# Encoder layer on one core: operands split in place, weights split later, loads re-placed at two stage borders

## The chip, the core and the metric

The kernel runs on one core of one Trainium2 chip. The metric is the device time of one execution in microseconds (us); lower is better. A core has TensorE (PE, with its weight loads as PEld), VectorE (DVE), ScalarE (ACT), GpSimd (POOL) and SyncE (SP), which here issues nearly all DMAs. Each engine runs its own instructions in the order in which they are written; semaphores make one engine wait for another.

## The reference

One transformer-like encoder layer on 2048 tokens of width 1024. `mlstm_group` is a bidirectional chunkwise mLSTM with 4 heads, `mla_group` a latent attention with 4 heads, and the feed-forward part squares a ReLU.

```python
z = rms_norm(x, g_mix) @ w_in                       # q, k, v, out-gate, gates | latents, rotary key
a = mlstm_group(q, k, v, o, gates, b_gates, g_out)  # sigmoid(o) * normed (forward + backward scan)
b = mla_group(c_q, c_kv, k_pe, cos, sin, ...)       # softmax(q k^T) v over all 2048 tokens
x = x + concat(a, b) @ w_out
x = x + square(relu(rms_norm(x, g_ffn) @ w1)) @ w2  # w1: 1024 x 4096, w2: 4096 x 1024
```

## The kernel before

**Arithmetic.** Every large product is made of three matmuls (`mm3`, lines 63 to 65). An operand is split (`split`, lines 48 and 49): ACT casts it to a rounded high part, DVE or POOL (`eng`) subtracts that from it for a low part. So each new operand tile costs an ACT instruction and a DVE or POOL instruction.

**Stages.** Projections (phase A, its order made by the framework's scheduler) run to about 465 us. From there on each engine's order is as the code is written. The attention loop makes one score product per step `g` and calls `next(work)` once per step, which advances the mLSTM generator (`mlstm_prelude`, `mlstm_steps`) by one `yield`; at its end `drain` (`OutProj.weights`) is advanced instead. Ahead of the loop stand the loads and splits of the first q block and the four k blocks of head 0 (`load_q`, `split_q`, `load_k`, `split_k`, POOL as `eng`). The output projection follows, then the feed-forward part.

**Phase A's last store.** `o` (the out-gate) is stored to `d_sg` from SP (line 454), 16 tiles in all.

**Attention's reciprocals.** `invert` takes the reciprocal of the row sums, writes them to DRAM (`d_rd`, line 1032) and at once loads them back broadcast over the partitions (`rb`, line 1034). SP waits for the store to land ahead of that load.

**Drain** (`weights`, from line 1176). `w_out` comes in 16 raw tiles through 8 stage buffers; ahead of `k == 4` the first two token tiles are loaded (`load_y`, `load_x`), into the ring, which has 8 buffers of one name `r`.

**Feed-forward, first layer** (`layer1`). A two-by-two Strassen scheme with 7 products: tokens come in two halves, `w1` in 16 blocks of 256 columns, so `n` runs from 0 to 31 with 7 products (slots) each; one product is 12 matmuls into a PSUM bank `pu` of 6. For a product, two operands must be there: 7 weight operands per `n` (`w1_split`; four of them combined by POOL from raw blocks, `w1_combine`, line 1358), and 7 token operands per half (`H`), each of four 128x512 pieces, which stay for 16 `n`. In a slot the order of the code is: product, stores, POOL combines of results (line 1452), `evacuate` of the product before it (DVE add, line 1415; ACT relu and square, lines 1418 and 1419), then for the next `n` combines and one split. Seven operands are split before the first product, two before and five behind `open1`.

**Second half of the tokens.** In `n` = 1 to 13 the generator `tokens`, one step per slot, normalises the tokens of the second half (ACT line 1287, POOL 59 and 1288, DVE 1291), transposes them on PE (`dpt`, lines 1300 and 1301), combines them (POOL, 1309) and stores all 7 operands to `d_h`. From `n` = 14 eight pieces are loaded into stage tiles, and in `n` = 15 and 16 `h_pieces` splits piece by piece into the operand tiles, as the first half's last products let go of them: 28 pieces of 128x512, several in one slot.

The second layer (7 products again, accumulated over `f`) is not touched.

## Time and profile before

| | us |
|---|---|
| median of 3 runs | 2686.47 (2686.41 to 2686.77) |
| profiled execution, its own time | 2682.24 |
| its span in the trace | 2680.5 |
| PE busy | 2599.5 (97%) |
| DVE busy | 1571.5 (59%) |
| ACT busy | 1196.0 (45%) |
| POOL busy | 806.6 (30%) |

The profiled execution is read by stretches: a view by windows gives for each the busy time of every engine and the granted TensorE clock. Shares over the whole span say little, since stages differ. The slices of the page in which PE is below nine tenths are four: the first, and those that hold 469 to 536, 1139 to 1206 and 1742 to 1809 us; the borders of the stretches shown further down were put where a stage's first and last instructions lie.

### The profile page before, as it was taken

What the parts mean: (1) busy time and instruction counts of PE and PEld (TensorE: products, weight loads), DVE (VectorE), ACT (ScalarE), POOL (GpSimd) and SP (SyncE); (2) the same over time, 40 slices, a digit from 0 to 9 for tenths busy, and PEclk for the clock granted to TensorE, in tenths of its full rate; (3) what the DMA queues carried; (4) which work ended last, traced back from release to release, by engine and by line L of the source; (5) the groups of instructions that cost most, each with busy time, mean ns of one, the idle gap of its engine ahead of it and who ended that gap; (6) DMA issues with size and microseconds to landing.
All of it is one profiled execution on the core that took longest, in us unless ns stands there. A gap on an engine that the chain in (4) does not pass through costs nothing. (4 is left out here: it accounts for less than half of the span.)

```text
span 2680.5 us, 37472 instructions
## 1 busy us (share of the span) xinstructions
PE 2599.5 (97%) x13227; PEld 2185.9 (82%) x13227; DVE 1571.5 (59%) x2918; ACT 1196.0 (45%) x2469; POOL 806.6 (30%) x738
## 2 busy tenths in 40 slices
PE   8999999899999999989999999989999999999999
PEld 6888887778888888878887777768887888888887
DVE  5585475555666666654366565665554377566443
ACT  6455443445656665652134444555444333322332
POOL 1211210223224232222216655555554023232000
PEclk9999999999999999999999999989999999999999
DMA  4344243255335343245665554654444844444552
GB/s 150 118 132 157 95 135 115 67 133 126 94 92 129 91 111 103 66 132 176 204 221 181 185 169 157 199 170 153 150 152 145 324 142 150 145 142 148 210 173 102
DMA packets 300599, 391.59 MB, mean 146 GB/s; under 512 B 33473, under 2 KB 187388, under 8 KB 300412
## 3 DMA queue, kind: packets, MB, share of 16 engines
q1 hardware_dynamic: 300412, 389.21, 46.3%
q8 instruction: 104, 1.70, 0.3%
q14 instruction: 83, 0.68, 0.1%
HBM read 256.94 MB, written 132.17 MB: 145 GB/s over the span
## 5 line engine op out<-in xcount | busy, mean ns | idle before, releaser
L63 PE MATMUL pd<-w2h,uh 128*128 128x512 f32 x896 | 349.3, 390 | 1.3 <-ACT w2h L48 1.0
L64 PE MATMUL pd<-w2l,uh 128*128 128x512 f32 x896 | 349.3, 390 | 0.9 <-DVE w2l L49 0.9
L65 PE MATMUL pd<-w2h,ul 128*128 128x512 f32 x896 | 349.1, 390 | 0.0
L49 DVE TENSOR_TENSOR ul<-ur,uh 128x1024 fp32r<-128x1024 f32 x110 | 152.7, 1388 | 257.3 <-ACT uh L48 257.3
L49 DVE TENSOR_TENSOR ptl<-ptp,pth 128x512 fp32r<-128x512 f32 x256 | 176.6, 690 | 200.2 <-ACT pth L48 200.1
L48 ACT CAST uh<-ur 128x1024 fp32r<-128x1024 f32 x110 | 115.9, 1054 | 396.0 <-PE pd L64 380.6
L49 DVE TENSOR_TENSOR r<-w1raw,r 128x512 fp32r<-128x512 f32 x160 | 153.5, 975 | 187.2 <-ACT r L48 187.1
L48 ACT CAST pth<-ptp 128x512 fp32r<-128x512 f32 x256 | 149.2, 583 | 254.3 <-PE ptp L1043 254.1
L1418 ACT ACTIVATE e<-e 128x512 f32<-128x512 f32 x128 | 80.9, 632 | 341.7 <-DVE e L1415 341.7
L1452 POOL TENSOR_TENSOR e<-e 128x512 f32<-128x512 f32 x128 | 188.9, 1485 | 126.1 <-ACT e L1419 117.1
L1015 DVE TENSOR_SCALAR_CACHE_REDUCE p<-ps 128x512 f32<-128x512 f32 x256 | 175.2, 684 | 58.9 <-PE ps L1014 57.9
L63 PEld LDWEIGHTS pd<-w2h,uh 128*128 128x128 f32 x896 | 168.3, 188 | 36.9 <-ACT w2h L48 1.4
L64 PEld LDWEIGHTS pd<-w2l,uh 128*128 128x128 f32 x896 | 168.3, 188 | 36.4 <-DVE w2l L49 1.6
L65 PEld LDWEIGHTS pd<-w2h,ul 128*128 128x128 f32 x896 | 168.3, 188 | 34.8
L1415 DVE TENSOR_TENSOR e<-pu,e 128x512 f32<-128x512 f32 x224 | 150.0, 681 | 23.4 <-PE pu L65 21.6
L1043 PE MATMUL ptp<-ident,p 128*128 128x128 f32 x1024 | 154.0, 274 | 0.0
L63 PE MATMUL pz<-wh,hh 128*128 128x512 f32 (+1 forms) x384 | 151.0, 395 | 3.0 <-ACT hh L48 3.0
L64 PE MATMUL pz<-wl,hh 128*128 128x512 f32 (+1 forms) x384 | 151.2, 394 | 0.4 <-DVE wl L52 0.3
L65 PE MATMUL pz<-wh,hl 128*128 128x512 f32 (+1 forms) x384 | 151.4, 394 | 0.0
L63 PE MATMUL pv<-pth,vh 128*128 128x256 f32 x512 | 146.0, 285 | 3.2 <-DVE y L1060 2.0
L1582 POOL TENSOR_TENSOR r<-wr,r 128x512 f32<-128x512 f32 x48 | 79.2, 1650 | 229.6 <-DMA wr<-in_w 149.0
L64 PE MATMUL pv<-ptl,vh 128*128 128x256 f32 x512 | 146.2, 286 | 1.4 <-DVE ptl L49 1.4
(361 smaller groups left out, 6807.2 us busy)
## 6 DMA issues: line engine op xcount, KB each, us to landing
d_u<-e SPq DMA_DIRECT2D x224, 256.0 KB, 2.3
ur<-d_u SPq DMA_DIRECT2D x110, 512.0 KB, 3.6
w1raw<-in_w SPq DMA_DIRECT2D x64, 512.0 KB, 4.7
wr<-in_w SPq DMA_DIRECT2D x96, 256.0 KB, 4.7
raw<-d_h SPq DMA_DIRECT2D x56, 256.0 KB, 4.3
raw<-in_w_in SPq DMA_DIRECT2D x48, 256.0 KB, 2.9
xt<-in_x SPq DMA_DIRECT2D x16, 512.0 KB, 3.6
mb<-d_M SPq DMA_DIRECT2D x32, 256.0 KB, 4.5
```

Of the source, the lines that this page charges most:

```text
L48: nc.scalar.copy(hi, src)
L49: (eng or nc.vector).tensor_tensor(lo, src, hi.bitcast(F32), op=ALU.subtract)
L63: nc.tensor.matmul(out, ah, bh, start=first, stop=False)
L64: nc.tensor.matmul(out, ah, bl, start=False, stop=False)
L65: nc.tensor.matmul(out, al, bh, start=False, stop=last)
L1015: nc.vector.tensor_scalar(probs[b, a][:, j, :], o, SCALE, None, op0=ALU.mult, op1=ALU.max, accum_out=maxes[b, a][:, j:j + 1])
L1043: nc.tensor.transpose(pt[:, k, :], p[:, j, k * P:(k + 1) * P], c.ident)
L1415: nc.vector.tensor_tensor(out, o, t, op=ALU.add)
L1418: nc.scalar.activation(t, t, AF.Relu)
L1452: self.c.nc.gpsimd.tensor_tensor(o, a, b, op=f)
L1582: nc.gpsimd.tensor_tensor(R, wr, R, op=ALU.subtract)
```

## The change

In phase A and the opening of attention: the `d_sg` stores are issued by ACT instead of SP; the first q block and k blocks 0, 1 and 3 are split with DVE instead of POOL; the prelude has two more yields ahead of its transposes, and two yields are taken out elsewhere. In attention, `invert` only stores, and a new `broadcast` loads four steps later. In the drain, `load_y` moves to `k` = 1 and 3, `load_x` to `k` = 6 and 7. The ring has two names, `r0` and `r1`, of 4 buffers each. In `layer1` a weight operand is split three products ahead of its use, ahead of the slot's evacuation; the combines of `w1` and its loads stand in other slots; only one operand instead of five is split behind `open1`; `tokens` has four yields instead of two between normalising and transposing. The second half's operands come by `exchange`: raw data is loaded into the tile of the low part, ACT copies it rounded to the high part, and DVE subtracts in place. Operand 0 uses the 8 stage tiles, operand 1 four ring tiles, and operands 2 to 6 the tiles of the first half's operands 0 to 4, loaded behind product (15, p). It has 4 pieces of 128x512 and 12 of 128x1024, one per slot, from `n` = 14 to 16.

```diff
-            nc.sync.dma_start(c.d_sg[t * P:(t + 1) * P, :], o)
+            nc.scalar.dma_start(c.d_sg[t * P:(t + 1) * P, :], o)
...
         nc.vector.tensor_copy(gs[:, 1:2], cu[:, P - 1:P])
         yield
+        yield
+        yield
...
         def invert(b):
             rd = dens[b]
             nc.vector.reciprocal(rd, rd)
+            nc.sync.dma_start(c.d_rd[b].rearrange("a p -> p a"), rd)
+
+        def broadcast(b):
             dd = c.d_rd[b]
-            nc.sync.dma_start(dd.rearrange("a p -> p a"), rd)
             rb = dens[b] = yp.tile([P, 256], F32, name="rb")
             nc.sync.dma_start(rb, bcast(dd.rearrange("a p -> (a p)"), P))
...
-        split_q(0, 0)
+        split_q(0, 0, nc.vector)
         for j in range(4):
             if j < 3:
                 load_k(0, j + 1)
-            split_k(0, j)
+            split_k(0, j, nc.gpsimd if j == 2 else nc.vector)
...
             if s == 2 and 0 < b <= N:
                 invert(b - 1)
+            if s == 6 and 0 < b <= N:
+                broadcast(b - 1)
...
-            if k == 4:
-                for s in range(2):
-                    self.load_y(s)
-                    self.load_x(s)
-                yield
+            if k in (1, 3):
+                self.load_y(k // 2)
+            elif k > 5:
+                self.load_x(k - 6)
...
     def w1_split(self, n, op):
-        w = self.ring.tile([P, 2, 4, P], F32R, name="r")
+        if (n, op) < (0, 2):
+            w = self.ring.tile([P, 2, 4, P], F32R)
+        else:
+            w = self.ring.pool.tile([P, 2, 4, P], F32R, name="r0")
...
+    def exchange(self):
...
+        def place(hi, lo):
+            nc.scalar.copy(hi, lo.bitcast(F32))
+            nc.vector.tensor_tensor(lo, lo.bitcast(F32), hi.bitcast(F32), op=ALU.subtract)
+
+        def load(hi, lo, src):
+            nc.sync.dma_start(lo.bitcast(F32), src)
+            todo.append((hi, lo))
+
+        first = [[self.stage.tile([P, 512], F32R, name="raw") for _ in range(4)] for _ in range(2)]
+        second = [[self.ring.pool.tile([P, 2, 512], F32R, name="r1") for _ in range(2)] for _ in range(2)]
...
+        for p in range(12):
+            if p < 5:
...
+                for k in range(0, 4, 2):
+                    load(hi[:, k:k + 2, :], lo[:, k:k + 2, :], c.d_h[1, p + 2, :, k:k + 2, :])
+            if p < 7:
+                self.H[p] = nxt[p]
+            place(*todo.pop(0))
+            yield
...
                 normalise(c, self.sp, x, x, [junk, junk])
-                yield
-                yield
+                for _ in range(4):
+                    yield
                 transpose_x(c, self.psT, x, x)
...
-                todo = [(op, k) for op in range(7) for k in range(4)]
-                for _ in range(8):
-                    self.h_load(1, *todo.pop(0))
-                extra = self.h_pieces(1, todo)
+                extra = self.exchange()
             for p in range(7):
                 self.product(n, p)
+                m, q = divmod(7 * n + p + 3, 7)
+                if m < N:
+                    self.w1_split(m, q)
                 self.flush()
...
                 prev = n, p, self.ps
-                if n + 1 < N:
-                    if p == 0:
-                        if n + 2 < N:
-                            self.load_w1(n + 2)
-                        self.w1_combine(n + 1, "S1")
-                        self.w1_combine(n + 1, "S2")
-                    elif p == 2:
+                if p == 0:
+                    self.w1_combine(n, "S4")
+                elif p == 1 and n + 1 < N:
+                    self.w1_combine(n + 1, "S1")
+                    self.w1_combine(n + 1, "S2")
+                elif p == 3:
+                    if n + 2 < N:
+                        self.load_w1(n + 2)
+                    if n + 1 < N:
                         self.w1_combine(n + 1, "S3")
-                    elif p == 4:
-                        self.w1_combine(n + 1, "S4")
-                    if p >= 1:
-                        self.w1_split(n + 1, p - 1)
-                    if p == 6:
-                        self.w1_split(n + 1, 6)
-                if n == 0 or (n == self.NU - 1 and p > 0) or n == self.NU:
-                    next(extra, None)
-                    next(extra, None)
-                    if n and p % 2 == 0:
-                        next(extra, None)
-                elif n < self.NU - 2:
+                next(extra, None)
+                if n == 0:
                     next(extra, None)
...
-                for k in range(2, 7):
-                    if k == 3:
-                        ff.w1_combine(0, "S4")
-                    ff.w1_split(0, k)
+                ff.w1_split(0, 2)
```

How the order moves at three places: first POOL at the opening of attention, between its last memset of the prelude (`v_4980`) and the split of v; `ql`, `kl` and `rl` are the low parts of q, k and the rotary part of k.

```order
 L542 MEMSET v_4980 128x4
-L49 TENSOR_TENSOR ql<-raw,qh 128x512
-L996 TENSOR_TENSOR qr<-raw,qr 64x512
-L49 TENSOR_TENSOR kl<-raw,kh 128x512
-L49 TENSOR_TENSOR rl<-raw,rh 128x512
-L49 TENSOR_TENSOR kl<-raw,kh 128x512
-L49 TENSOR_TENSOR rl<-raw,rh 128x512
-L49 TENSOR_TENSOR kl<-raw,kh 128x512
-L49 TENSOR_TENSOR rl<-raw,rh 128x512
 L49 TENSOR_TENSOR kl<-raw,kh 128x512
 L49 TENSOR_TENSOR rl<-raw,rh 128x512
 L49 TENSOR_TENSOR vl<-raw,vh 128x512 x4
```

Eight subtracts leave POOL; the pair that stays is that of k block 2. On DVE they stand among phase A's last instructions.

Second, SP in the drain, before: `raw` are tiles of `w_out`, `d_ya` and `d_yb` the two halves of the projection's input.

```order
L1184 DMA raw<-in_w_out 128x512 x4
L1032 DMA d_rd<-rd_13181 128x2x1
L1034 DMA rb<-d_rd 128x256
L1184 DMA raw<-in_w_out 128x512 x2
L1063 DMA d_yb<-y 128x256
L1184 DMA raw<-in_w_out 128x512 x2
L1222 DMA r<-d_ya 128x512
L1223 DMA r<-d_yb 128x4x128
```

The same place in the changed kernel:

```order
L1198 DMA raw<-in_w_out 128x512 x2
L1235 DMA r_13345<-d_ya 128x512
L1236 DMA r_13345<-d_yb 128x4x128
L1198 DMA raw<-in_w_out 128x512 x2
L1031 DMA d_rd<-rd_13179 128x2x1
L1198 DMA raw<-in_w_out 128x512 x2
L1065 DMA d_yb<-y 128x256
L1235 DMA r_13401<-d_ya 128x512
L1236 DMA r_13401<-d_yb 128x4x128
L1198 DMA raw<-in_w_out 128x512 x2
L1036 DMA rb<-d_rd 128x256
```

The first `d_ya` load now stands ahead of the store of `d_rd`, and the load of `rb` stands six loads and a store behind that store instead of right behind it.

Third, DVE in `layer1` at the first token tile, before: L1291 is the normalising multiply, L1301 the copy of the transposed tile out of PSUM, L49 the low part of a weight operand, and L1415 an evacuation.

```order
L1291 TENSOR_SCALAR raw<-raw,nr 128x512 x2
L1415 TENSOR_TENSOR e<-pu,e 128x512 x2
L49 TENSOR_TENSOR r<-sw,r 128x512
L1415 TENSOR_TENSOR e<-pu,e 128x512
L49 TENSOR_TENSOR r<-w1raw_15056,r 128x512 x2
L1301 TENSOR_TENSOR raw<-dpt,vec 128x512 x2
L1415 TENSOR_TENSOR e<-pu,e 128x512
```

The same place in the changed kernel (L1304 is the multiply, L1470 the evacuation, L1314 the copy):

```order
L1304 TENSOR_SCALAR raw<-raw,nr 128x512 x2
L49 TENSOR_TENSOR r_15311<-sw,r_15311 128x512
L1470 TENSOR_TENSOR e<-pu,e 128x512 x2
L49 TENSOR_TENSOR r_15331<-w1raw_15112,r_15331 128x512
L1470 TENSOR_TENSOR e<-pu,e 128x512
L49 TENSOR_TENSOR r_15351<-w1raw_15110,r_15351 128x512
L1470 TENSOR_TENSOR e<-pu,e 128x512
L49 TENSOR_TENSOR r_15372<-sw,r_15372 128x512
L1314 TENSOR_TENSOR raw<-dpt,vec 128x512 x2
```

Between the multiply and the copy stand four slots' work instead of two; splits and evacuations alternate as they did.

## Rows read from the trace of the kernel before

**Rows 1.** Windows: stretch; its us; PE, PEld, DVE, ACT, POOL busy (instructions); clock; DMA share; GB/s

```profile
465.50:500.70 35.20, 23.02 (x89) 16.25 (x89) 19.04 (x56) 14.91 (x21) 18.23 (x19) 0.81 0.38 102
1169.30:1199.00 29.70, 18.89 (x119) 16.86 (x116) 16.55 (x31) 17.98 (x35) 12.37 (x10) 0.83 0.61 179
1387.00:1711.90 324.90, 305.63 (x1326) 248.07 (x1325) 199.51 (x251) 148.06 (x272) 193.86 (x157) 0.97 0.53 174
1711.90:1731.20 19.30, 19.30 (x86) 15.78 (x85) 12.84 (x14) 9.81 (x18) 10.63 (x7) 1.00 0.51 156
1731.20:1773.30 42.10, 30.69 (x86) 19.45 (x85) 34.00 (x42) 23.34 (x44) 14.57 (x9) 0.76 0.60 192
1773.30:2063.30 290.00, 290.00 (x1261) 236.84 (x1259) 158.82 (x208) 137.64 (x241) 159.33 (x116) 1.00 0.44 151
...
1653.85:1673.18 19.33, 19.33 (x85) 15.80 (x85) 11.96 (x16) 9.25 (x16) 11.01 (x8) 1.00 0.46 155
```

**Rows 2.** Waits, 440 to 505 us: who waits for whom, total, times, longest

```profile
PE ps L1011 <- POOL kl L49: 5.2, 2, 4.8
...
PE pm L592 <- DVE gs L587: 4.9, 1, 4.9
...
PE ps L1010 <- DVE p L1015: 1.1, 1, 1.1
```

**Rows 3.** Timeline of SP's queue: start, us, instruction

```profile
445.14 22.96 SPq L454 DMA_DIRECT2D d_sg<-vo  x5
468.20 0.38 SPq L952 DMA_DIRECT2D raw<-d_kn  x1
```

**Rows 4.** Timeline of POOL at the opening of attention

```profile
468.96 1.26 POOL L49 TENSOR_TENSOR kl<-raw,kh 128x512 fp32r<-128x512 f32 x1
...
477.59 1.28 POOL L49 TENSOR_TENSOR rl<-raw,rh 128x512 fp32r<-128x512 f32 x1
```

**Rows 5.** Waits, 1169 to 1200 us

```profile
PE pm L1239 <- DMA r<-d_ya: 6.1, 1, 6.1
```

**Rows 6.** Timeline of SP's queue in the drain

```profile
1177.23 0.43 SPq L1032 DMA_DIRECT2D d_rd<-rd  x1
1185.04 0.33 SPq L1034 DMA_DIRECT2D rb<-d_rd  x1
...
1188.10 0.37 SPq L1222 DMA_DIRECT2D r<-d_ya  x1
```

**Rows 7.** Waits, 1387 to 1711 us

```profile
ACT e L1418 <- DVE e L1415: 157.8, 57, 7.8
DVE r L49 <- ACT r L48: 107.8, 58, 5.0
...
PE dpt L1300 <- DVE raw L1291: 19.3, 11, 5.3
DVE raw L1291 <- POOL nr L59: 17.4, 8, 4.0
...
ACT r L48 <- POOL w1raw L1358: 12.5, 3, 5.6
```

**Rows 8.** Timelines of ACT, then DVE, then POOL, 1656 to 1676 us

```profile
1656.14 0.60 ACT L48 CAST r<-sw 128x512 fp32r<-128x512 f32 x1
...
1674.90 0.60 ACT L48 CAST r<-sw 128x512 fp32r<-128x512 f32 x1
...
1656.77 0.69 DVE L49 TENSOR_TENSOR r<-sw,r 128x512 fp32r<-128x512 f32 x1 [1.27 <-ACT r L48]
...
1669.39 1.74 DVE L49 TENSOR_TENSOR r<-w1raw,r 128x512 fp32r<-128x512 f32 x1 [1.88 <-ACT r L48]
...
1669.29 1.29 POOL L1452 TENSOR_TENSOR e<-e 128x512 f32<-128x512 f32 x1
```

**Rows 9.** Groups of DVE's instructions, 1711 to 1773 us: busy, mean ns, idle before

```profile
L49 DVE TENSOR_TENSOR h0l<-raw,h0h 128x512 fp32r<-128x512 f32 x4 | 5.9, 1506 | 0.0
...
L49 DVE TENSOR_TENSOR h5l<-raw,h5h 128x512 fp32r<-128x512 f32 x4 | 2.6, 680 | 0.0
```

More of the change, by code (lines that the diff above doesn't have):

```diff
@@ L956, in load_k, with split_k @@
             kraw[h, j] = raw, rr
-        def split_k(h, j):
+        def split_k(h, j, eng=nc.gpsimd):
             raw, rr = kraw.pop((h, j))
@@ L961, in split_k @@
             kl = kp.tile([P, 512], F32R, name="kl")
-            split(nc, kh, kl, raw, eng=nc.gpsimd)
+            split(nc, kh, kl, raw, eng=eng)
             rh = kp.tile([P, 512], F32R, name="rh")
             rl = kp.tile([P, 512], F32R, name="rl")
-            split(nc, rh, rl, rr, eng=nc.gpsimd)
+            split(nc, rh, rl, rr, eng=eng)
             K[h, j] = kh, kl, rh, rl
@@ L987, in load_q, with split_q @@
             qraw[h, j] = raw, rr
-        def split_q(h, j):
+        def split_q(h, j, eng=nc.gpsimd):
             raw, rr = qraw.pop((h, j))
@@ L992, in split_q @@
             ql = qp.tile([P, 512], F32R, name="ql")
-            split(nc, qh, ql, raw, eng=nc.gpsimd)
+            split(nc, qh, ql, raw, eng=eng)
             qr = qp.tile([P, 512], F32R, name="qr")
             nc.scalar.copy(qr, rr)
-            nc.gpsimd.tensor_tensor(qr[ROPE:P, :], rr[ROPE:P, :], qr[ROPE:P, :].bitcast(F32),
-                                    op=ALU.subtract)
+            eng.tensor_tensor(qr[ROPE:P, :], rr[ROPE:P, :], qr[ROPE:P, :].bitcast(F32), op=ALU.subtract)
             Q[h, j] = qh, ql, qr
@@ L1160, with __init__, tile @@
 UOP = {p[0]: i for i, p in enumerate(PROD2)}
+class Ring:
+    def __init__(self, pool):
+        self.pool, self.n = pool, 0
+    def tile(self, shape, dtype):
+        self.n += 1
+        return self.pool.tile(shape, dtype, name=f"r{self.n % 2}")
 class OutProj:
@@ L1189, in weights @@
         yield
-        self.yp = self.ent_ring(c.tc.tile_pool(name="ring", bufs=8, side="right", reuse_waits="tile"))
+        self.yp = Ring(self.ent_ring(c.tc.tile_pool(name="ring", bufs=4, side="right", reuse_waits="tile")))
         self.wp = self.ent_w(c.tc.tile_pool(name="o_w", bufs=1, side="right", reuse_waits="tile"))
@@ L1219, in load_y @@
         tok = slice(t * P, (t + 1) * P)
-        y = self.yp.tile([P, 2, 512], F32, name="r")
+        y = self.yp.tile([P, 2, 512], F32)
         ya, yb = y[:, 0, :], y[:, 1, :].rearrange("p (k t) -> p k t", k=NH)
@@ L1228, in load_x @@
         t = self.ORDER[s]
-        xt = self.x[s] = self.yp.tile([P, D], F32, name="r")
+        xt = self.x[s] = self.yp.tile([P, D], F32)
         nc.sync.dma_start(xt, c.x[t * P:(t + 1) * P, :])
@@ L1234, in prep_y @@
         ya, yb = self.y.pop(s)
-        yh = self.yp.tile([P, 8, P], F32R, name="r")
-        yl = self.yp.tile([P, 8, P], F32R, name="r")
+        yh = self.yp.tile([P, 8, P], F32R)
+        yl = self.yp.tile([P, 8, P], F32R)
         pt = bank if bank is not None else self.psY.tile([P, 4, P], F32, name="ypt")
@@ L1375, in h_split @@
             pool = self.hp if op < 3 else self.hp1
-            self.H[op] = (pool.tile([P, 4, 512], F32R, name=f"h{op}h"),
-                          pool.tile([P, 4, 512], F32R, name=f"h{op}l"))
+            t = [pool.tile([P, 4, 512], F32R, name=f"h{op}{part}") for part in "hl"]
+            self.H[op] = [[x[:, i, :] for i in range(4)] for x in t]
         hh, hl = self.H[op]
-        split(self.c.nc, hh[:, k, :], hl[:, k, :], raw)
+        split(self.c.nc, hh[k], hl[k], raw)
+    def exchange(self):
+        c, nc = self.c, self.c.nc
+        todo = []
+        def place(hi, lo):
[6 more added lines that the diff above has]
+        second = [[self.ring.pool.tile([P, 2, 512], F32R, name="r1") for _ in range(2)] for _ in range(2)]
+        for k in range(4):
+            load(first[0][k], first[1][k], c.d_h[1, 0, :, k, :])
+            if k % 2:
+                yield
+        for k in range(2):
+            load(second[0][k], second[1][k], c.d_h[1, 1, :, 2 * k:2 * k + 2, :])
+        yield
+        for _ in range(4):
+            place(*todo.pop(0))
+            yield
+        nxt = [first, [[t[:, k, :] for t in s for k in range(2)] for s in second]]
+        for p in range(12):
+            if p < 5:
+                pool = self.hp if p < 3 else self.hp1
+                hi, lo = (pool.tile([P, 4, 512], F32R, name=f"h{p}{part}") for part in "hl")
+                nxt.append([[t[:, k, :] for k in range(4)] for t in (hi, lo)])
+                for k in range(0, 4, 2):
+                    load(hi[:, k:k + 2, :], lo[:, k:k + 2, :], c.d_h[1, p + 2, :, k:k + 2, :])
+            if p < 7:
+                self.H[p] = nxt[p]
+            place(*todo.pop(0))
+            yield
     def h_pieces(self, g, todo):
@@ L1403, in product @@
         for k in range(4):
-            mm3(self.c.nc, o, wh[:, k, :], wl[:, k, :], hh[:, k, :], hl[:, k, :], k == 0, k == 3)
+            mm3(self.c.nc, o, wh[:, k, :], wl[:, k, :], hh[k], hl[k], k == 0, k == 3)
     def slots(self, n):
@@ L1476, in tokens @@
                 normalise(c, self.sp, x, x, [junk, junk])
-                yield
-                yield
+                for _ in range(4):
+                    yield
                 transpose_x(c, self.psT, x, x)
```

## The prediction

> **What bounds the kernel now.** I read the windows first, because the span's mean hides the weak places: PE is busy 97% of it. The reader is to see three stretches in which PE is not full [rows 1]: the opening of attention (465.5 to 500.7, PE 23.02 of 35.2 us at a clock of 0.81), the drain (1169.3 to 1199.0, PE 18.89 of 29.7 us), and the first 17 of 32 steps `n` of the first feed-forward layer (1387.0 to 1773.3, three rows). A step that nothing disturbs takes 19.33 us with PE busy throughout [rows 1], and the 15 later steps take 290.0 us, just 15 times that. The first 17 should then take 17 x 19.33 = 328.6 us; they take 324.9 + 19.3 + 42.1 = 386.3, 57.7 more. PE also makes 64 transposes for the tokens in them. A matmul of 512 columns takes 19.33 / 84 = 0.23 us here and a transpose has a quarter of the columns, so they are worth between 0.06 and 0.23 us each, 4 to 15 us; I take 6.4, near the lower end (an estimate). About 51 us is then idle or slowed time.
>
> Then the waits, stretch by stretch. In the opening PE waits 5.2 us in two waits for POOL's `kl` and 4.9 for `gs` [rows 2]. POOL starts its first `kl` only at 468.96 and ends its last `rl` at 477.59 + 1.28 = 478.87 [rows 4], while SP stands 22.96 us at five `d_sg` stores and issues the next k load at 468.20 [rows 3]. In the drain PE waits 6.1 us for the first `d_ya` tile [rows 5]; SP issues that load at 1188.10, after standing from the `d_rd` store (1177.23) to the `rb` load behind it (1185.04) [rows 6].
>
> In the feed-forward part PE's named waits are for the normalised token (19.3 us, 11 times), which suggests that the transposes come too early. But the same list has no entry of DVE or ACT waiting for PE: the evacuation, which must wait for PE if PE is the bound, never does. ACT waits for DVE's add 157.8 us, DVE for ACT's cast 107.8 [rows 7]. So I read the two as one chain, handing a tile back and forth (cast, subtract, add, relu and square, next cast). From one `n` to the next, the cast of `sw` comes 1674.90 - 1656.14 = 18.76 us later [rows 8], just under PE's 19.33. Seventeen steps of it are 318.9 us, so 386.3 leaves 67.4 us that tokens, exchange and waits put into it. PE stalls only where the lag of this chain shows.
>
> **The opening.** Removed from POOL: three k pairs and the q pair, 8 subtracts of about 1.26 us [rows 4]; they go to DVE among the last work of phase A, at about 0.69 us each [rows 8], 5.5 us beside a full PE. The `d_sg` stores leave SP, so the k and v loads come before the stage rather than at 468.20 [rows 3]. Added to ACT: 16 issues of about 0.33 us [rows 6], 5 us over the whole of phase A, which ACT hides; behind a store there that waits for DVE stands ACT's own next cast, which the PE would see only through phase A's buffers. The weight split there can delay PE; I put 0 to 2 us on that, inside my bound. What is left in the opening: PE's busy 23.02 us at clock 0.81 is 18.6 at full clock. The two `kl` waits (5.2) go. The `gs` wait (4.9) has two more steps ahead of it; at 18.6 / 12 = 1.55 us of PE work in a step (an estimate: some 12 steps stand ahead of the first product with v) 1.8 remain. The wait for a score bank (1.1) [rows 2] may grow as PE comes to it sooner, and so may those behind it in the prelude; I leave 3.3 us for them together. 18.6 + 1.8 + 3.3 = 23.7, so **11.5 us** gained of 35.2; bounds 8 and 14 (the `gs` wait stays whole and the clock half recovers; or the banks cost nothing).
>
> The Trainium skill, page "DMA: Bandwidth & Descriptors", section "Issuing engines are not separate DMA queues", says that issuing from another engine saves only the sequencer's time of issuing; by it moving `d_sg` would be worth nothing here. The row says otherwise for a queue in which a store waits for its data: SP stood 22.96 us at five of them [rows 3].
>
> **The drain.** SP's 7.8 us between 1177.23 and 1185.04 [rows 6] go, and the `d_ya` load stands ahead of the store. PE's wait of 6.1 us [rows 5] then ends by the data before it. What is late next is ACT: it is busy 17.98 of the 29.7 us [rows 1], with 16 casts of `w_out` and the last softmax casts, and cannot end much before 20 us even if it waits only 2. The stretch would go from 29.7 to 22.7, some 3 us above that floor, since the last transposes still wait for it: **7 us**; bounds 3 (the wait moves to ACT) and 9.7 (the floor). The old cover of `broadcast`: it comes four steps later, and the output that uses `rb` is several steps behind it; in the tail of the drain this is the tightest place, and it is inside the lower bound.
>
> **Layer 1, part by part.** Each slot keeps one cast, one subtract and one evacuation, and the split stands ahead of the evacuation instead of behind it. The ring cast, subtract, add, relu, square, cast is the same, and the third piece of order says so: `L49` and `L1470` alternate. So I leave the chain at 18.76 us a step and count what leaves it.
> - The combines now come three or more products ahead of the split that needs them, not about two; ACT's 12.5 us of waits for a POOL combine [rows 7] should go nearly all: 10 us.
> - Four fewer splits stand ahead of the first steps. A split is a cast of 0.60 and a subtract of 0.69 [rows 8], 1.3 us, 5.2 in all, of which I count 3 as exposed at the stage's border. They are not saved, only made later, where PE has a margin.
> - The chain need not have caught up at `n` = 16. The 15 steps behind have 0.57 us of slack each, 8.6 us; I count 4 (an estimate) of it as newly used.
> - The tokens' two more yields move PE's transposes and change nothing in the chain: DVE's wait of 17.4 us for POOL's `nr` [rows 7] stays, because the multiply stands where it stood. What is late next at PE is then a weight, now only three products ahead: it shows after 3 x 2.76 = 8.3 us of lag instead of about 16.
> - The exchange has the same 14,336 columns per partition to cast and subtract; with 1024 columns in one instruction and one in a slot, fewer collide with POOL: 0 to 8 us. I take 0. Its loads wait on SP for product (15, p); queued behind them there are the stores of results and the next `w1` block, both several products early.
>
> 10 + 3 + 4 = **17 us**. The bounds: the combines' gain can be lost to contention (-5), or the waits that I call symptoms may partly be causes (30).
>
> **The sum.** 11.5 + 7 + 17 = 35.5 us. The profiled execution took 2682.24 us; 2682.2 - 35.5 = 2646.7. The median of the runs, 2686.47, is 4.2 above it, so the forecast is 2651.
>
> **Rivals.** *The waits are the bound.* If the chain's rate is not fixed (DVE's 17.4 us for `nr` and the bursts of splits being causes), moving the transposes and spreading the exchange recover all 51 us: 2686.5 - 11.5 - 7 - 51 = 2617. For it speaks that PE names exactly these instructions [rows 7] and that the exchange stretch alone is 42.1 - 19.3 = 22.8 us long; against it, that no evacuation waits for PE. Chance 0.13.
>
> *Nothing comes back in layer 1.* The three-product lead gives PE's stalls to weights, and the combines' wait turns into another; opening and drain alone give 2686.5 - 18.5 = 2668. The form of it in which the change doesn't do what it says belongs here: k block 2 is still POOL's, and ACT may stand behind a `d_sg` store, so that opening and drain give 0 to 5, and the time is within 0.2% of before. Chance 0.18 together, a third of it for the latter.
>
> *The chain becomes longer than PE's step: slower.* A DVE subtract that meets a POOL instruction takes 1.74 us instead of 0.69 [rows 8], and the pieces of operand 0 took 1506 ns against 680 for operand 5 [rows 9]. The change puts other POOL combines beside other subtracts in all 32 steps. Chain 18.76 against 19.33 leaves 0.57 us; one more collision in each step (1.05 us) makes 19.8, two make 20.9. With 32 steps, the kernel loses more than the 35.5 us gained elsewhere from 19.33 + 35.5/32 = 20.4 us a step, and at 20.9 it loses 50: 2686.5 - 35.5 + 50 = 2701. Chance 0.08. The Trainium skill, page "SBUF: State Buffer", section "SBUF: two separate sides", states that DVE and POOL share a port pair that the first holds for its whole instruction while the other fully blocks. The rows agree: the 1.74 us subtract ended 0.55 us after POOL's instruction [rows 8].
>
> **How the numbers follow.** The forecast holds 0.61, with a range of its own of 2633 (14 + 9.7 + 30 gained) to 2676 (8 + 3 + 0, since not all three fall to their lower bound together). The range for all, 2622 to 2676, reaches half way to the first rival and past the second's 2668; left out are the slower rival, the "does not do it" case and half of the first rival, 0.2 together. A measurement of this kernel can tell about 0.2%, 5.4 us, from no change. Faster by more: 0.61 + 0.13 + 0.12 = 0.86; within: 0.06; slower by more: 0.08.
>
> **What would show each step.** In the changed kernel's trace: no wait of PE for `kl` of POOL and an opening of about 24 us; no wait for `d_ya`, a drain of 22 to 23 us; in layer 1 ACT's waits for POOL's combines gone, PE's waits now for weights, still no evacuation that waits for PE, and the first 17 steps at about 369 us. Were evacuations to wait for PE there, and the 17 steps near 335, the first rival would be right. Steps behind `n` = 17 above 19.33 us would show the last rival, and make the prediction wrong.

## The result and the profile after

The changed kernel took 2667.59 us (median of 4 runs, 2663.33 to 2670.84), the kernel before 2686.62 beside it. The ratio is 0.9928, 95% interval 0.9911 to 0.9945: faster by 19 us, and inside the range of the prediction, but some 17 us short of its centre. The profiled execution took 2668.72 us, 13.5 less than that of before. The kernel before had medians from 2681.8 to 2686.6 in the different batches of runs, so below I compare ratios within a batch, and stretches within a trace.

Windows of the changed kernel, columns as in [rows 1]. The first four rows stand for the opening, the drain, and `n` = 0 to 16 in two parts; then come the 15 later steps, and the 17 steps in one row:

```profile
466.30:490.60 24.30, 18.48 (x84) 14.33 (x85) 18.65 (x54) 13.94 (x19) 8.46 (x11) 0.93 0.35 97
1158.30:1188.80 30.50, 19.50 (x123) 17.08 (x121) 17.47 (x32) 18.34 (x39) 12.55 (x10) 0.83 0.71 177
1376.80:1697.60 320.80, 306.57 (x1325) 246.41 (x1324) 205.41 (x245) 147.02 (x271) 199.31 (x156) 0.98 0.53 172
1697.60:1759.00 61.40, 47.69 (x169) 33.67 (x168) 44.79 (x48) 31.46 (x48) 28.23 (x17) 0.92 0.63 205
1759.00:2049.00 290.00, 290.00 (x1261) 236.62 (x1259) 187.07 (x209) 138.16 (x242) 172.16 (x117) 1.00 0.44 144
1376.80:1759.00 382.20, 354.26 (x1493) 280.08 (x1492) 250.20 (x292) 178.48 (x319) 227.55 (x172) 0.97 0.54 177
```

The opening went from 35.2 to 24.3 us, and phase A ends 0.8 later, so 10.1 are won at its end. From the last score product to the first product of the output projection it is 30.5 us, and by the same two marks 30.3 before: nothing. The first 17 steps went from 386.3 to 382.2, 4.1 us. Each other stretch is the same to 1 us, but in the attention loop (from the first product with v to the last score product, 668.0 us before and 667.7 after) that is a loss and a gain in one. PE's idle time ahead of the mLSTM's outer product fell, by rows of before and of after (`issue` is time in which the engine waits for nothing that the profile shows):

```profile
PE pm L691 <- issue: 6.5, 16, 1.2
```

```profile
PE pm L693 <- issue: 1.4, 5, 0.3
```

And just behind the opening's window PE waits for `y`, which waits for `rb`, now loaded later; before, no such wait stands in the loop:

```profile
DVE y L1062 <- DMA rb<-d_rd: 6.4, 1, 6.4
...
PE pv L63 <- DVE y L1062: 5.6, 1, 5.6
```

In the eleven later traces with the changed attention (all below but e4) PE's wait for `y` there is 0.7 to 2.3 us, and the loop takes 661 to 663. So the profiled execution seems to show some 5 us less than the change wins as a rule, which is about what lies between its 13.5 us and the 19 of the medians; a second trace of the changed kernel itself would have to show it. Where the prediction had 11.5, 7 and 17, the trace has 10.1, 0 and 4.

One row tells more than these. In the 15 later steps PE is full in both kernels, but DVE is busy 187.07 us, against 158.82 before [rows 1], for the same instructions. The waits of 1376 to 1678 us (who waits for whom: total, times, longest), 14 steps, which answer to the 15 of [rows 7]:

```profile
ACT e L1473 <- DVE e L1470: 155.2, 53, 9.1
DVE r L49 <- ACT r L48: 81.8, 49, 2.1
...
DVE raw L1304 <- POOL nr L59: 25.2, 8, 4.2
...
PE pu L65 <- DVE r L49: 13.3, 7, 4.0
```

ACT's waits for a combine of POOL are gone, as are PE's for the normalised token. PE now waits for a weight's low part. That is the pattern I expected, yet the time is nearly the same, because the chain itself became slower. ACT's casts of `sw` one step apart (timeline: start, us):

```profile
1851.52 0.62 ACT L48 CAST r<-sw 128x512 fp32r<-128x512 f32 x1
...
1871.03 0.61 ACT L48 CAST r<-sw 128x512 fp32r<-128x512 f32 x1
...
1890.53 0.62 ACT L48 CAST r<-sw 128x512 fp32r<-128x512 f32 x1
```

A step of the chain takes 19.51 us, where [rows 8] had 18.76. That is more than PE's 19.33: from `n` = 17 to 31 the evacuations fall 0.18 us further behind in each step, which the six banks hide until the end. Groups of DVE's subtracts in steps 17 to 30 (busy, mean ns | idle before), before and then after:

```profile
L49 DVE TENSOR_TENSOR r<-w1raw,r 128x512 fp32r<-128x512 f32 x70 | 67.5, 979 | 85.4 <-ACT r L48 85.4
L49 DVE TENSOR_TENSOR r<-sw,r 128x512 fp32r<-128x512 f32 x29 | 25.9, 895 | 19.1 <-ACT r L48 19.1
```

```profile
L49 DVE TENSOR_TENSOR r<-w1raw,r 128x512 fp32r<-128x512 f32 x70 | 85.2, 1217 | 70.3 <-ACT r L48 70.3
L49 DVE TENSOR_TENSOR r<-sw,r 128x512 fp32r<-128x512 f32 x27 | 34.6, 1283 | 26.2 <-ACT r L48 26.2
```

A subtract alone takes 0.69 us [rows 8]. Where it meets POOL it looks like this in the changed kernel (timelines of DVE, then POOL):

```profile
1865.20 1.78 DVE L49 TENSOR_TENSOR r<-w1raw,r 128x512 fp32r<-128x512 f32 x1
...
1863.43 3.00 POOL L1507 TENSOR_TENSOR e<-e 128x512 f32<-128x512 f32 x2 [3.74 <-ACT e L1474]
```

It ends 0.55 us behind POOL's second instruction, as in [rows 8]. So the theory with which I went into the experiments: one chain of DVE and ACT bounds the first half of layer 1 in both kernels, and POOL's combines, which the change moved, lengthen it. Its rivals: the place of the split in the slot lengthens it; or PE's stalls have other causes (tokens, exchange) and the chain is a symptom.

### The profile page after: what moved, and what is told of

It reads as the page before. It is cut to its first block, busy times and chain, and to the rows that moved or that the text cites. A ratio compares the mean times of both kernels' runs of the same rounds, so it can differ in the third digit from the quotient of the medians.

```text
span 2666.9 us, 37134 instructions
## 1 busy us (share of the span) xinstructions
PE 2594.1 (97%) x13227; PEld 2180.9 (82%) x13227; DVE 1615.9 (61%) x2914; ACT 1193.9 (45%) x2457; POOL 826.3 (31%) x730
## 5 line engine op out<-in xcount | busy, mean ns | idle before, releaser
L49 DVE TENSOR_TENSOR ul<-ur,uh 128x1024 fp32r<-128x1024 f32 x110 | 146.9, 1336 | 253.7 <-ACT uh L48 253.5
L49 DVE TENSOR_TENSOR ptl<-ptp,pth 128x512 fp32r<-128x512 f32 x256 | 176.7, 690 | 193.8 <-ACT pth L48 193.7
L49 DVE TENSOR_TENSOR r<-w1raw,r 128x512 fp32r<-128x512 f32 x160 | 187.6, 1173 | 140.8 <-ACT r L48 140.8
L1473 ACT ACTIVATE e<-e 128x512 f32<-128x512 f32 x128 | 80.9, 632 | 346.8 <-DVE e L1470 346.8
L1507 POOL TENSOR_TENSOR e<-e 128x512 f32<-128x512 f32 x128 | 183.4, 1443 | 120.8 <-ACT e L1474 118.2
L1629 POOL TENSOR_TENSOR r<-wr,r 128x512 f32<-128x512 f32 x48 | 87.0, 1813 | 223.3 <-DMA wr<-in_w 141.0
L1470 DVE TENSOR_TENSOR e<-pu,e 128x512 f32<-128x512 f32 x224 | 149.6, 680 | 1.4 <-POOL e L1507 1.2
```

The costliest lines, as they stand in the source:

```text
L49: (eng or nc.vector).tensor_tensor(lo, src, hi.bitcast(F32), op=ALU.subtract)
L1470: nc.vector.tensor_tensor(out, o, t, op=ALU.add)
L1473: nc.scalar.activation(t, t, AF.Relu)
L1507: self.c.nc.gpsimd.tensor_tensor(o, a, b, op=f)
L1629: nc.gpsimd.tensor_tensor(R, wr, R, op=ALU.subtract)
```

## The experiments

**The chain's length.** First the split behind the evacuation again:

```diff
-                if m < N:
-                    self.w1_split(m, q)
...
                 if prev:
                     self.evacuate(*prev)
...
+                if m < N:
+                    self.w1_split(m, q)
```

> The changed kernel with one thing put back: in each slot the weight split stands behind the evacuation again. In the changed kernel the lag of the evacuations behind PE grows by 0.18 us per n from n = 17 to 31, so the chain of DVE and ACT takes 19.33 + 0.18 = 19.51 us per n there; it took 18.76 before. Theory (DVE's subtracts meet POOL's combines more often: 1217 ns instead of 979 for the subtract of a raw weight): the place of the split in the slot changes little, the mean stays above 1100 ns, the lag does not shrink by more than 0.3 us per n, and the time is within 8 us of the changed kernel's 2667.6. Rival (the split ahead of the evacuation makes the hand-off longer): back to 18.76 us per n, the lag shrinks by 0.57 us per n, and the first 17 steps take some 13 us less than 382.2, so about 2655.

2672.17 us, ratio 0.9961 (0.9947 to 0.9976). The subtracts took 1279 and 1253 ns in steps 17 to 30, and the 17 steps 384.0 us. Steps 17 to 31 took 294.6, 4.5 more than in the changed kernel. The rival fell: the order inside the slot did not lengthen the chain, putting it back costs a little. Then the changed kernel without the combines of `w1` from `n` = 2 on, which leaves that part of the computation out:

```diff
     def w1_combine(self, n, name):
...
-        self.c.nc.gpsimd.tensor_tensor(...)
+        if n < 2:
+            self.c.nc.gpsimd.tensor_tensor(...)
```

> The changed kernel without POOL's combines of w1 from n = 2 on (that part of the computation is left out; the splits work on the raw blocks as they are). Theory (contention of DVE's subtracts with POOL sets the chain): the mean subtract falls below 950 ns, the chain to 18.5 us per n or less, the evacuations catch up with PE before n = 31, the first 17 steps take 360 to 372 us instead of 382.2, and the time is 2645 to 2658. Rival (the chain is longer for its order): subtracts and the growth of the lag by 0.18 us per n stay, and the time is within 5 us of 2667.6.

2640.48 us, ratio 0.9843 (0.9829 to 0.9858), 17 steps in 360.3 us, and from `n` = 19 on the lag (from the end of a product to its evacuation) constant, 1.3 to 2.8 us by the slot. So four POOL instructions in a step, for which no cast or subtract of the changed kernel is seen to wait long, cost 22 us of the first 17 steps. Three numbers missed: the subtracts still took 1091 and 1033 ns, not under 950, with the four combines of results still there; the evacuations didn't catch up with PE; and the time lies 4.5 us under the range. Does the place of the combines matter? First those of `w1` moved back:

```diff
-                if p == 0:
+                if p == 0 and n == 0:
                     self.w1_combine(n, "S4")
-                elif p == 1 and n + 1 < N:
-                    self.w1_combine(n + 1, "S1")
-                    self.w1_combine(n + 1, "S2")
-                elif p == 3:
+                if p == 3:
...
                     if n + 1 < N:
-                        self.w1_combine(n + 1, "S3")
+                        self.w1_combine(n + 1, "S1")
+                        self.w1_combine(n + 1, "S2")
+                elif p == 5 and n + 1 < N:
                     self.w1_combine(n + 1, "S3")
+                elif p == 6 and n + 1 < N:
+                    self.w1_combine(n + 1, "S4")
```

> The changed kernel with the combines of w1 in other slots (S1 and S2 in slot 3, S3 in slot 5, S4 in slot 6, so that POOL no longer does six of its eight combines in slots 0 to 2); the hand-off is coupled as in the changed kernel. Theory (where the combines stand decides how many subtracts meet them): the mean subtract falls from 1144 and 1230 ns to 1050 or less, the lag no longer grows behind n = 17, and the first 17 steps take 365 to 376 us, time 2650 to 2662. Rival (only how much POOL does counts, not where): mean above 1100 ns, time within 6 us of 2667.6. Against the theory: the split of S2 now stands two slots behind its combine, and ACT may wait for POOL there.

2677.22 us, ratio 0.9979 (0.9969 to 0.9988), slower than the changed kernel by 0.5%. The mean subtract fell from 1144 and 1230 ns (in the first 17 steps and in the later ones) to 1076 and 1079, not to 1050 as the theory asked; behind `n` = 17 the lag grew by 0.38 us a step, where the theory had it stand still; and a new wait took more than the shorter subtracts gave:

```profile
ACT r L48 <- POOL sw L1371: 23.6, 8, 7.0
```

The 17 steps took 393.6 us: two slots between combine and cast are too few when POOL is behind. So I moved the other four, which nothing waits for soon:

```diff
-                    if p == 1:
+                    if p == 3:
                         self.u_combine(n - 1, "S1")
                         self.u_combine(n - 1, "S2")
-                    elif p == 2:
+                    elif p == 4:
                         self.u_combine(n - 1, "S3")
-                    elif p == 3:
+                    elif p == 5:
                         self.u_combine(n - 1, "S4")
```

> The changed kernel with POOL's combines of results moved from slots 1, 1, 2, 3 to slots 3, 3, 4, 5, so that POOL's eight combines of a step are no longer nearly all in slots 0 to 3; no split waits for these. Theory (where the combines stand decides how many subtracts meet them): mean subtract 1080 ns or less (1144 and 1230 in the changed kernel), the lag no longer grows behind n = 17, the first 17 steps 366 to 377 us instead of 382.3, time 2650 to 2663. Rival (only how much POOL does counts): mean above 1100 ns, the lag grows as before, time within 5 us of 2667.6.

2661.18 us, ratio 0.9922 (0.9908 to 0.9937), which by ratio is the changed kernel again. The subtracts of steps 17 to 30, and DVE's waits in the first 14 steps:

```profile
L49 DVE TENSOR_TENSOR r<-w1raw,r 128x512 fp32r<-128x512 f32 x71 | 63.8, 898 | 80.6 <-ACT r L48 80.4
L49 DVE TENSOR_TENSOR r<-sw,r 128x512 fp32r<-128x512 f32 x28 | 27.7, 988 | 40.0 <-ACT r L48 40.0
```

```profile
DVE r L49 <- ACT r L48: 85.8, 59, 3.0
...
DVE raw L1304 <- POOL nr L59: 26.2, 8, 4.0
...
DVE e L1470 <- POOL e L1507: 8.4, 5, 2.4
```

The subtracts are as short as before the change (984 and 936 ns over all of them in the two parts), and the lag behind `n` = 17 no longer grows (2.4 to 2.9 us): where POOL's work stands does decide how long the chain is there. But the first 17 steps took 380.8 us, not 366 to 377. DVE's wait for `nr` there is what it was (25.2 us after the change); new are some 8 us of waits for POOL's combines of results. What else the shorter subtracts went into stays open. So the collisions explain the later steps; in the first 17 they are not shown to cost much. The time by trace is 7.7 us below that of the changed kernel, but 5.7 of that stand ahead of layer 1, where the two kernels are the same.

**The chain itself.** If one serial hand-off is the bound, cutting it must win more than any of this. ACT's cast stays ahead of the evacuation and DVE's subtract goes behind it (`w1_split` with `True` makes the cast and returns the subtract):

```diff
-                if m < N:
-                    self.w1_split(m, q)
+                sub = self.w1_split(m, q, True) if m < N else None
...
                     self.evacuate(*prev)
...
+                if sub:
+                    sub()
```

> The changed kernel with the hand-off cut in layer 1: in each slot ACT's cast of the weight stands ahead of the evacuation, as it does, and DVE's subtract behind it, so that DVE adds while ACT casts, and neither waits for the other twice in a slot. Theory (one serial chain of cast, subtract, add, relu and square bounds layer 1): the first 17 steps fall from 382.2 to 345 to 360 us, the evacuations stay within about 3 us of PE from n = 18 on, and the time is 2630 to 2648. Rival (PE's stalls come from the tokens' waits and the late exchange loads, not from the chain): within 5 us of 2667.6.

2626.88 us (2626.40 to 2628.09), ratio 0.9795 (0.9779 to 0.9812). The 17 steps took 345.9 us, and from `n` = 18 to 30 the evacuations stayed within 0.7 us of PE; the time was 3 us below what the theory gave. Windows of `n` = 0 to 13 and 14 to 16, and waits in the first:

```profile
1370.50:1648.20 277.70, 277.70 (x1242) 227.64 (x1241) 181.31 (x236) 146.02 (x258) 188.46 (x149) 1.00 0.57 187
1648.20:1716.40 68.20, 62.55 (x253) 49.07 (x252) 51.59 (x57) 40.07 (x62) 38.43 (x24) 0.95 0.69 232
```

```profile
ACT r L1380 <- PE pu L65: 82.2, 58, 3.1
...
ACT e L1480 <- DVE e L1477: 37.9, 23, 4.4
DVE e L1477 <- PE pu L65: 34.2, 35, 1.5
```

PE is full for 277.7 us, and DVE's evacuations wait for PE 35 times. No such wait stood in [rows 7] or after the change. 14 steps of 19.33 are 270.6, so the tokens' transposes cost 7.1 us, near the 6.4 estimated. The cut also shortened the subtracts, from a mean of 1142 ns in the first 14 steps to 942; but e11 had 968 there and took 380.8 us for the 17, so it is the hand-off that counts and not the length of the subtracts. The same cut in the kernel before:

> The kernel before with the same cut in layer 1 and nothing else: casts ahead of the evacuation, subtracts behind it. Theory: the chain was the bound there too, so the first 17 steps fall from 386.3 to 350 to 368 us and the time from 2686.5 to 2652 to 2670. Rival (there the transposes that came too early and the crowded exchange were the bound): the 17 steps stay above 380 and the time above 2680.

The edit is that of e3, for the splits of that kernel. 2647.75 us, ratio 0.9871 (0.9857 to 0.9886), 17 steps in 350.7 us instead of 386.3; the time lies under the theory's range by as much as the kernel before ran faster in this batch (2682.19). The transposes and the crowded exchange stood there unchanged, so they were not the bound: one hand-off was worth 35.6 us in the kernel before, and 36.4 in the changed one (382.3 to 345.9). With it cut, `n` = 14 to 16 take 68.2 us with the new exchange and 70.0 with the old; coupled it was 80.9 and 80.7. The same cut in the exchange, where `finish` subtracts the piece before:

```diff
         def place(hi, lo):
+            finish()
             nc.scalar.copy(hi, lo.bitcast(F32))
-            nc.vector.tensor_tensor(lo, lo.bitcast(F32), hi.bitcast(F32), op=ALU.subtract)
+            behind.append((hi, lo))
```

> The kernel e3_cast_ahead with the same cut made in the exchange: a piece's in-place subtract stands one slot behind its ACT copy, so DVE no longer waits for the copy in the slot. Theory (in the exchange too the hand-off adds up: add, relu, square, copy, subtract in a row are longer than a product): n = 14 to 16 take 60 to 65 us instead of 68.2, time 2619 to 2625. Rival (ACT and DVE are simply full there, 2.8 to 2.9 us of work in a slot of 2.76): 67 us or more, time within 2 us of 2626.9.

2621.96 us (2620.03 to 2627.42), ratio 0.9784 (0.9767 to 0.9801); `n` = 14 to 16 in 63.8 us, of which three steps of PE are 58:

```profile
1647.00:1710.80 63.80, 60.55 (x254) 48.02 (x253) 53.26 (x58) 41.33 (x64) 40.25 (x24) 0.97 0.72 252
```

The step is clear in the trace; by the ratios (0.9795 and 0.9784) it is inside the noise. It is the fastest kernel of this study with e12, below.

**The opening**, on e3. The stores of `d_sg` back on SP, splits as changed:

```diff
-            nc.scalar.dma_start(c.d_sg[t * P:(t + 1) * P, :], o)
+            nc.sync.dma_start(c.d_sg[t * P:(t + 1) * P, :], o)
```

> The kernel e3_cast_ahead with the d_sg stores back on SP, the splits still on DVE. Theory (SP standing at those stores was what kept the k loads back): SP stands some 20 us again, PE waits 3 us or more for k, and the first product with v comes 5 to 10 us later than e3's 488.9, so the time is 2632 to 2637. Rival (the place of the splits alone made the gain): within 2 us of e3's 2626.9.

2627.18 us, ratio 0.9785: no difference, the rival was right. SP stands at the stores as before:

```profile
446.01 16.66 SPq L454 DMA_DIRECT2D d_sg<-vo  x4
464.17 0.57 SPq L658 DMA_DIRECT2D v<-d_v  x1
```

But no k load is behind them: the last load of `d_kn` leaves at 417.76 us, ahead of the stores (468.20 in the kernel before). Then the splits back on POOL:

```diff
-        split_q(0, 0, nc.vector)
+        split_q(0, 0)
-            split_k(0, j, nc.gpsimd if j == 2 else nc.vector)
+            split_k(0, j)
```

> The kernel e3_cast_ahead with the splits of the first q and k blocks back on POOL, the d_sg stores still on ACT. Theory (POOL stands at its memset of qz until the last projection, at about 466 us, so its splits start there however early the data came): PE waits 2 us or more for kl, the first product with v comes 3 to 8 us later than e3's 488.9, time 2630 to 2635. Rival (only the late loads mattered): within 2 us of e3's 2626.9.

2632.08 us, ratio 0.9806 (0.9789 to 0.9822). Against e6, in the same batch, it is 4.9 us slower. The first product with v comes at 497.8 instead of 488.9, 1 us later than the theory's range; counted from phase A's last product it is 33.9 us, against 24.3 and 25.2 in e3 and e6. The last k load leaves late again, at 465.65 us, though no `d_sg` store stands ahead of it on SP: SP's queue waits for POOL's `ql`, which lets go of the buffer. And PE's old wait is there:

```profile
SPq L953 <- POOL ql L49: 22.1, 1, 22.1
```

```profile
PE ps L1011 <- POOL kl L49: 5.3, 2, 4.8
```

So the engine of the splits decides when the k loads leave, not the stores. In the kernel before the same `ql` ended at 467.21 us, 1 us ahead of the load [rows 3]; more the stores can't have cost there:

```profile
465.95 1.26 POOL L49 TENSOR_TENSOR ql<-raw,qh 128x512 fp32r<-128x512 f32 x1
```

By the traces of e7 and e3, 8.9 us at the opening have shrunk to 5.3 at the end. Where the rest went isn't shown: the drain is 1.9 us shorter in e7, but the same code takes 29.0 to 30.9 us there in the nine traces that have it.

**The drain.** In the changed kernel PE's wait there, and what ACT waits for:

```profile
PE pv L63 <- ACT pth L48: 7.4, 3, 6.2
...
ACT woh L48 <- DMA raw<-in_w_out: 5.9, 3, 2.7
```

The last softmax cast (`pth`) stands on ACT behind casts of `w_out` whose data is late:

```profile
1177.38 0.62 ACT L48 CAST woh<-raw 128x512 fp32r<-128x512 f32 x1 [2.65 <-DMA raw<-in_w_out]
...
1182.38 1.27 ACT L48 CAST woh<-raw 128x512 fp32r<-128x512 f32 x2 [2.50 <-DMA raw<-in_w_out]
1183.55 0.58 ACT L48 CAST pth<-ptp 128x512 fp32r<-128x512 f32 x1
```

So, on e3:

```diff
             elif k > 5:
+                if k == 6:
+                    yield
+                    yield
                 self.load_x(k - 6)
```

> The kernel e3_cast_ahead with two more yields in the drain ahead of k = 6, so that the last softmax cast stands ahead of the last four casts of w_out on ACT. Theory (in the changed drain the last product with v waits 6.2 us for a cast that is queued on ACT behind casts of w_out, whose data came 2.65 and 2.50 us late): PE's wait for that cast goes below 1 us, the stretch from the last score product to the first output projection falls from 30.9 us to 25 to 28, and the time is 2 to 6 us below e3's 2626.9. Rival (the transfers themselves are the bound, 5.5 MB in 30 us): the wait moves to the output projection's first tiles, and the time stays within 1.5 us of e3's.

The wait went, and PE waited for `y` instead:

```profile
PE ypt L1255 <- DVE y L1062: 6.0, 1, 6.0
```

27.9 us instead of 30.9 (29.0 to 30.9 in the traces of the unchanged drain), but 2626.94 us, ratio 0.9786, no gain. I took the late broadcast of the last reciprocals for the cause, and replaced its store and load by a matmul of ones with a diagonal, on top of e9 and the two yields:

```diff
...
+            if b == NH * NB - 1:
+                o = psM.tile([P, 512], F32, name="pm")[:, 0:256]
+                nc.tensor.matmul(o, t[:, 0, 0:P], t[:, 1, 0:256], start=True, stop=True)
+                nc.vector.tensor_copy(rb, o)
+                return
```

> The kernel e9_place_behind with the two yields of e5 in the drain, and the last block's reciprocals broadcast by a matmul of ones with a diagonal tile instead of by a store to d_rd and a load. Theory (in e5 PE's wait for the last cast had gone, and in its place PE waited 6.0 us for y, since the store of d_rd took 9.8 us to land among the drain's loads and rb came only after it): that wait goes, the stretch from the last score product to the first output projection falls to 21 to 25 us from e5's 27.9, and the time is 3 to 6 us below e9's. Rival (the transfers are the bound): the output projection's first products wait for w_out or for d_ya instead, and the time is within 1.5 us of e9's.

That reading was wrong. 2623.64 us, ratio 0.9780, a stretch of 28.7 us, and PE still waits for `y`. DVE's timeline of e5 had shown why:

```profile
1178.14 0.69 DVE L49 TENSOR_TENSOR wol<-raw,woh 128x512 fp32r<-128x512 f32 x1 [3.45 <-ACT woh L48]
1179.35 1.34 DVE L49 TENSOR_TENSOR r<-r,r 128x512 fp32r<-128x512 f32 x1 [0.52 <-ACT r L48]
1180.61 0.68 DVE L49 TENSOR_TENSOR r<-pm,r 128x512 fp32r<-128x512 f32 x1
1181.21 0.41 DVE L1062 TENSOR_TENSOR y<-pv,rb 128x256 f32<-128x256 f32 x1
```

`y` starts as soon as DVE is done with the subtracts ahead of it, and the first of those waited 3.45 us for ACT. Four yields on e9 move part of them behind `y`:

```diff
+                if k == 6:
+                    for _ in range(4):
+                        yield
```

> The kernel e9_place_behind with four yields in the drain ahead of k = 6 and nothing else there. In e5 and e10 the last y stood on DVE behind the subtracts of w_out and of the first token tile, which waited for ACT's casts and those for w_out's data; here y stands ahead of the last of them. Theory (the order on ACT and DVE holds PE in the drain, not the transfers): from the last score product to the first output projection 24 to 27 us instead of e9's 29.3, time 2617 to 2620. Rival (transfers are the bound; what is won at the stage's border is given back in the output projection, where PE then waits for w_out or d_ya): time within 2 us of e9's 2622.

26.4 us instead of 29.3, as the theory said. The median is 2622.30 (2618.45 to 2626.73), ratio 0.9775 (0.9762 to 0.9788), not told apart from e9's. PE still waits 4.4 us for `y`, and now `y` does wait for `rb`:

```profile
DVE y L1062 <- DMA rb<-d_rd: 3.8, 1, 3.8
```

So the order on ACT and DVE held some 3 us of the drain, and the late `broadcast` is what is late next. The two were not taken away together, and how much of PE's other idle time there is the transfers' stayed open.

## Why the prediction was right or wrong

**The opening: right in size, wrong in part of its reason.** 10.1 us against 11.5. The `kl` and `gs` waits went, but the wait for a score bank grew from 1.1 [rows 2] to 4.1 us. With 1.1 for `mr` and 0.7 for `vo` PE waits 5.9 us, where the forecast left 5.1 (1.8 and 3.3):

```profile
PE ps L1010 <- DVE p L1015: 4.1, 1, 4.1
```

I argued from [rows 3] that the `d_sg` stores kept the k loads back, and set that against the Trainium skill's page "DMA: Bandwidth & Descriptors" (section "Issuing engines are not separate DMA queues"), by which another issuing engine saves only the time of issuing. e6 agrees with the page: with the splits on DVE, the stores on SP cost nothing. What kept the k load back was its buffer, which POOL's `ql` held (22.1 us of SP's waits in e7). The split's engine carries the gain (9.5 us of the opening, e7 against e3). The term for `broadcast` was looked for in the drain only; the 5.6 us wait for `y` behind the opening is its price in this execution, and the forecast had nothing for it.

**The drain: wrong.** The step that failed is "what is late next is ACT ... cannot end much before 20 us", made from ACT's busy time. Busy time left out what ACT would wait for: casts in its queue wait for `w_out`, behind two token tiles that now load ahead of part of it, and the last softmax cast is queued behind them. With that order changed (e12), the late `rb` came next, which the forecast held inside its lower bound. PE's 6.1 us for `d_ya` [rows 5] became 6.2 for that cast.

**Layer 1: the bound was named rightly, the step "I leave the chain at 18.76 us a step" failed.** e3 and e4 confirm the chain, and the waits that PE showed were symptoms: it now waits for weights instead, as said. But the chain takes 19.51 us a step in the later steps. If that holds for the first 17 too, 17 x 0.75 = 12.8 us are lost, which is what lies between the 17 forecast and the 4.1 measured; e11 shows that it doesn't hold so simply, since shorter subtracts alone gave back only 1.5 us there. What is shown: the combines of `w1` cost 22 us of the first 17 steps (e2); their share in the difference between the two kernels is argued, not shown, and where the missing 13 us of the first 17 steps went stays open. The exchange, taken as 0, was 0 as long as the hand-off stood.

**The rivals.** The mechanism of the slower one came true at less than its price: a chain above PE's step, from DVE and POOL colliding. It decided from 20.4 us a step and reached 19.51. I gave it as an all-or-nothing case with 0.08 and kept it out of the forecast's sum; as a term with a bound of, say, half a collision in a step it would have taken off 9 us (17 x 1.05 / 2). The measured time lies at the second rival's 2668, but by chance: that is the sum of opening and drain without layer 1, and the drain gave nothing. The first rival's 2617 was nearly reached by e9, by cutting the hand-off, not by moving transposes.

**The sum.** 35.5 forecast, 13.5 by the traces, 19 by the medians. Of the three terms one held; that the time lies in the range is owed to the range's width, and to the attention loop, which had no term: there PE's idle time ahead of the outer product fell by 5 us (6.5 to 1.4). The opening's bounds also don't follow from what is said for them: with the `gs` wait whole (3.1 more) and half of the clock (2.2 more) 6.2 us are left, not 8, and without the banks it is 14.8, not 14. The 4.2 us by which I set the median above the profiled execution did not stay: after the change the profiled one is 1.1 above its median.

## What to carry to other kernels

When the engine that should be the bound waits for another in named places, but nobody waits for it, look for a ring of two other engines: its time per step, from one instruction to the same one a step later, is the number to compare with the bound's. Cut the ring (issue the first half of a pair early, the second half behind what lies between) before moving what waits; here that was worth 36 us in both kernels, and moving instructions 4. When a queue's order is changed, cost what each moved instruction will wait for, not only how long it takes. And before one trace each is read for what an edit did, see how far the same code differs between traces: here 29.0 to 30.9 us in the drain, and 661 to 668 in the attention loop.

## What the runs showed of the hardware

The collisions of DVE and POOL go with longer instructions on both sides. In layer 1 of the changed kernel, counted instruction by instruction, a subtract of a weight that overlaps no combine of POOL took 720 ns in the mean (84 of them), one that does 1467 (138); a combine took 1298 alone (70) and 1580 beside such a subtract (179). The combine `sw` of two raw blocks took 1317 ns in the first part of layer 1 before, and in the changed kernel:

```profile
L1371 POOL TENSOR_TENSOR sw<-w1raw,w1raw 128x512 f32<-128x512 f32 x15 | 24.7, 1645 | 5.0 <-DVE r L49 5.0
```

With the same eight POOL instructions in a step, the mean of a raw block's subtract in steps 17 to 30 was 979, 1217, 898 and 901 ns (before, after, e11, e3). The amount of work on the two engines hardly differs between these; only when it is issued does.
